# A hybrid S5 / RWKV-7 layer on one core: weight parts made by two streams, S5 matrices set up earlier, v convolved on TensorE, gate blocks moved

## Chip, cores and metric

The kernel runs on one core of a Trainium2 chip. The metric is the device time of one execution in microseconds. A core has five engines: TensorE (PE, with its weight loads as PEld), VectorE (DVE), ScalarE (ACT), GpSimd (POOL) and SyncE (SP, which here issues nearly all DMAs).

## The reference

One layer over a latent stream x (512 tokens of 1024) and a context stream ctx (256 tokens) that share all weights, in fp32. Only x is returned; of the context only the end states of the two recurrences are used.

```python
x   = half_ffn(x,   mod_x, 0, ...)      # SwiGLU, FFN_DIM 2816, x + 0.5*mod*y
ctx = half_ffn(ctx, mod_c, 0, ...)
hc, hx = modulate(ctx, ...), modulate(x, ...)
_, ctx_states = token_mixers(hc, 1, zeros, p, False)
out_x, _ = token_mixers(hx, rows, ctx_states, p, True)
x = x + mod_x[5] * out_x
x = half_ffn(x, mod_x, 2, ...)
return rmsnorm(x, final_g)
```

Inside token_mixers (cut): one product with w_in gives the S5 input u, the RWKV r, k, v, the low-rank inputs of decay and rate, and two gates.

```python
ya = s5_scan(u, forward) + s5_scan(u, backward) + D * u      # 32 groups, 64 complex states
rkv = centred_conv(rkv, conv, rows)          # 3x3 per channel on 8 rows of 64 tokens (context: 1 row)
S = S*w + (S@aa) x bb + v x k ; yb = S@r     # RWKV-7, 8 heads of 64, both directions
ya = gelu(ya); ya = ya * sigmoid(ya @ w_glu)
yb = (group_norm(yb) + bonus) * g @ w_o
out = (sigmoid(gate_a) * (ya @ w_proj) + sigmoid(gate_b) * yb) @ w_out
```

## The kernel before

**Products.** Every weight tile (128 x 1024 fp32, `raw`) comes by DMA and is split in two fp32r parts: `wh` is a rounded copy made on ScalarE, `wl = raw - wh` a subtraction on VectorE or GpSimd. The activations are split alike (`hx` of the latents, `hc` of the context, `ah`/`al` of the FFN's hidden values), and each product is three matmuls (`mm3`): hi x wh, lo x wh, hi x wl. In the instruction rows hx_109 and hx_110 are the two parts of the latents. All products stand in one list, `items`: context FFN, latent FFN with the context's w_in products (`win`) between, w_in of the latents, 16 gate blocks, then glu, wo, proj, wout, and the second FFN. `dense` (line 352) walks through the list. Before each item it calls `w_split` (line 328) until the item's tiles and some more (`WLA`, or 2) are split, so casts and subtractions are issued from within the stream of products.

**Order.** The program is written by a planner, `Plan` (line 61), a list scheduler with a cost for each kind of operation. Each stage is a generator, a stream with a priority; at each `yield` it names what it needs next (tiles, or events that another stream posts), and `run` takes the first stream by priority that is ready by the plan's clock. Every operation is issued from one helper (line 209), so that all rows of the profile have that line and are told apart by tile. `shared` (line 103) keeps one list of intervals in which VectorE and GpSimd use a common port, and lays operations of both after each other.

**Stages.** `phase_a` runs the modulation products (w_mod), both first FFNs and, in `ctx_run` (line 908), the context's mixers. `s5_build` (line 955) computes the S5 transfer matrices: powers of the state matrix on VectorE, 96 products and sums on GpSimd (tiles ms, X), others on VectorE (mh, H), then 16 rounds on TensorE, each with four transposes of X and four products of X with cb, copied out on ScalarE and stored by DMA (GTd, Kd). It is added as a stream in `ctx_run`, after the context FFN. The context recurrence needs its event `s5b`. `rw_pre`, `rw_main` (lines 1577, 1641) do RWKV in chunks: steps 0 to 3 for the context, 4 to 11 for the latents (tiles T, tt, M, w, R, Z, bt); `s5_rec` (line 1747) the S5 recurrence on GpSimd, four small operations a chunk.

**Before the recurrence of the latents.** `conv_evac` and `conv` (lines 1229, 1243) make the 3x3 convolution: each w_in product of r, k, v is copied into a zeroed 10x66 tile `pad`, scaled by the centre tap, and eight scalar-tensor-tensor operations on VectorE add the other taps (tiles cvr, cvk, cvv). `pa` and `pb` (lines 1291, 1371) make the chunk operands: nb, kt, st.

**After it.** `s5_out`, then `s5_post`: yi is loaded back, gelu gives `yg`, on which `glu_mm` (line 1888) waits. Of the 16 gate blocks the last four stand after glu (`GLUP`). `wo_mm` and `proj_mm` (lines 1874, 1906) work on halves of the tokens; each loads its gate tile `gt` (two buffers) just before its products.

Of the kernel before, what the change touches and what calls it, by code (L numbers as in the profile page):

```python
# [17 lines left out]
FT = 22  # L18
# [10 lines left out]
SPD = 0  # L29
WOL = 4  # L30
S5V = 600
S5Q = 3000
MPV = 1200
SPLIT_AT = 0
S5P = 3
# [6 lines left out]
WLA = 4  # L42
GLUP = 4
# [8 lines left out]
class Plan:  # L52
# [8 lines left out]
    def __init__(self, nc):  # L61
# [5 lines left out]
        self.port, self.shape = [], None  # L67
# [35 lines left out]
    def shared(self, t, cost):  # L103

        self.port = [i for i in self.port if i[1] > min(self.free["V"], self.free["P"])]
        for a, b in self.port:
            if t + cost <= a:
                break
            t = max(t, b)
        self.port = sorted(self.port + [(t, t + cost)])  # L110
        return t

    def step(self, e, cost, out, ins, work=0.0, port=False):
# [4 lines left out]
        if port:  # L118
            t = self.shared(t, cost)
# [153 lines left out]
class Reg:  # L273


    def __init__(self, v, n, p0):
# [4 lines left out]
        self.cv, self.kn, self.pd, self.cvq, self.n_conv = {}, {}, {}, [], 0  # L281


class Kern:
# [43 lines left out]
    def w_split(self):  # L328

        nc, i = self.nc, self.n_split  # L330
        if i == len(self.items):
            return
        s = next((s for s in self.slots if i < self.end[s[0]]), None)
        if s is None:
            return
        if i not in self.raw:
            self.w_loads(1)
        self.n_split += 1
        nb = self.items[i][1]
        r, sr = self.raw.pop(i)  # L340
        self.slots.remove(s)
        wh, wl = (s[0].tile([128, 8, 128], F32R, name=n, tag=f"{n}{s[1]}") for n in ("wh", "wl"))
        nc.scalar.copy(wh[:, :nb], r[:, :nb])
        f = self.sch.free
        late = max(f["P"], self.sch.t) + 2300 > max(f["V"], self.sch.t) + 1150
        eng = nc.vector if (i < self.n_post + 2 or i >= self.n_ffn) and late else nc.gpsimd
        eng.tensor_sub(wl[:, :nb], r[:, :nb], wh[:, :nb].bitcast(F32))
        if sr[0] not in self.gone:
            self.raws.append(sr)
        self.wsp[i] = (wh, wl, s)  # L350

    def dense(self):
# [3 lines left out]
        while i < len(self.items):  # L356
# [3 lines left out]
            while self.n_split < i + n:  # L360
                self.w_split()
            self.w_loads()
            la = WLA if self.n_post <= i < self.n_ffn else 2
            for _ in range(la):
                if self.n_split < i + n + la:
                    self.w_split()
            yield list(self.wsp[i][:2])
            ws = [self.wsp[j][:2] for j in range(i, i + n)]
# [8 lines left out]

    def parts(self, px, ws, h, spec):

        for s, ks, c, needs in spec:  # L380
            yield needs + list(ws[s])
# [17 lines left out]
    def build(self):  # L399
        nc, tc, a, es = self.nc, self.tc, self.a, self.es  # L400
        self.X, self.C = X, C = Reg(0, NX, 4), Reg(1, NCT, 0)
        self.raw, self.wsp, self.n_load, self.n_split, self.late = {}, {}, 0, 0, None
# [49 lines left out]
        self.items[i] += (["b2"],)  # L452
        self.n_post = len(self.items)
# [32 lines left out]
    def mods01(self):  # L486
# [11 lines left out]
        def loaded(n):  # L498
# [6 lines left out]
            if n == 12:  # L505
                self.w_loads(2)
            if n == 16:
                self.w_loads()

        def step(n):  # L510
            if n >= 6:
                next(st0, None)
            if n >= 13:
                self.w_split()
# [245 lines left out]
    def tail(self, l, r, ws):  # L760
# [8 lines left out]
        def half(s, c):  # L769
            px = self.dbank()[:, :256]  # L770
            wh, wl = ws[s]
            yield [wh, wl]
# [59 lines left out]
    def down_half(self, l, r, ws, b):  # L832

        nc, v, c = self.nc, r.v, r.half[b]
        for q in range(KT // 2):
            wh, wl = ws[q // 2]
            yield [wh, wl, self.hid[FT - 1][1]]
# [22 lines left out]
    def phase_a(self):  # L860
        nc, a, sch, X, C = self.nc, self.a, self.sch, self.X, self.C
        with ExitStack() as es:
# [4 lines left out]
            C.h = [hcp.tile([128, KT, NCT], F32R, name=f"hc{i}") for i in range(2)]  # L867
            wrs, self.wxr = self.right("wxr")
# [8 lines left out]
            sch.add(self.dn, 9)  # L877
            sch.run(*st)
# [29 lines left out]
    def ctx_run(self, es, wrs):  # L908
# [3 lines left out]
        X.fp = es.enter_context(self.pool("fpx"))  # L912
        sch.post("fp0x")
# [6 lines left out]
        self.cas.close()  # L920
# [1218 lines left out]
```

## Time and profile before

| | us |
|---|---|
| runs | 1901.99, 1898.08, 1900.58 (median 1900.58) |
| profiled execution, its own time | 1891.72 |
| its span | 1890.0 |
| TensorE busy, share | 1672.3, 88% |
| VectorE | 996.4, 53% |
| ScalarE | 716.9, 38% |
| GpSimd | 687.5, 36% |
| mean granted TensorE clock | 0.939 of full speed |

The stages along the span, by the tiles in the trace: 0 to 109 us modulation products; 109 to 273 context FFN; 273 to 857 latent FFN, with the S5 set-up, the context's w_in and preparation, and the context recurrence between; 857 to 1082 w_in of the latents, convolution, pa and pb; 1082 to 1351 gates and latent recurrence; 1351 to 1531 glu, gates, wo, proj, wout; from 1531 the second FFN and the last norm. A share of busy time over the span is a mean over these; the stages are read one by one.

### The profile page before, as it was taken

To read this page: it belongs to the slowest core of one execution; us is meant where nothing else is said; L and a number is where in the kernel's file an instruction comes from. 1 tells how busy PE (TensorE), PEld (TensorE's weight loads), DVE (VectorE), ACT (ScalarE), POOL (GpSimd) and SP (SyncE) were. 2 spreads that over 40 slices of the span, in tenths; PEclk is the share of its full clock that TensorE was granted. 3 is DMA by queue.
4 is the path that set the end of the run, shared out by engine and by line. 5 is a ranking of instruction groups with operands and counts; after the bars stand their busy time and mean duration, and the time that the engine had idled before them with its cause. 6 is when DMAs were issued, how large, how long until landed. Compare 5 with 4: busy or idle time off the path is not lost.

```text
span 1890.0 us, 33157 instructions
## 1 busy us (share of the span) xinstructions
PE 1672.3 (88%) x13208; PEld 1400.3 (74%) x13208; DVE 996.4 (53%) x1747; ACT 716.9 (38%) x1200; POOL 687.5 (36%) x815
## 2 busy tenths in 40 slices
PE   6889999999999988778976789968697999999996
PEld 3689987778878867665544567758587988888886
DVE  3376564755558728355788855643343433333335
ACT  3355442545463212535443333443443332222222
POOL 0144231555764314621334537660065421111111
PEclk9999999999999999888988889979799999999998
DMA  9955541335454474433753566466364223323231
GB/s 310 331 167 195 183 155 57 113 106 159 143 160 140 141 190 151 119 123 128 252 160 105 148 223 188 118 172 176 123 215 159 67 69 101 99 91 101 98 101 56
DMA packets 235626, 278.43 MB, mean 147 GB/s; under 512 B 93616, under 2 KB 186800, under 8 KB 234448
## 3 DMA queue, kind: packets, MB, share of 16 engines
q1 hardware_dynamic: 235472, 276.32, 47.8%
q8 instruction: 104, 1.70, 0.4%
q14 instruction: 50, 0.41, 0.1%
HBM read 234.31 MB, written 43.22 MB: 147 GB/s over the span
## 4 chain that ended last, share of the span: by engine, by line
PE 56%; DVE 14%; DMA 14%; ACT 6%; issue 4%; POOL 3%; SPq 3%; DVEq 0%; ACTq 0%; POOLq 0%
PE b L209 56%; DMA wmod<-in_wmod 3%; SPq L209 3%; POOL wl L209 2%; ACT wh L209 2%; DMA Hd<-H 2%; DMA raw<-in_wgu 2%; DVE st L209 1%; DVE mh L209 1%; DVE wl L209 1%; DMA gt<-gates 1%; DVE rs L209 1%; DVE prod L209 1%; DVE cvr L209 1%; DVE H L209 1%
## 5 line engine op out<-in xcount | busy, mean ns | idle before, releaser
L209 PE MATMUL b<-hx,wh 128*128 128x512 f32 (+1 forms) x2432 | 698.2, 374 | 22.6 <-ACT wh L209 10.9
L209 POOL TENSOR_TENSOR wl<-raw,wh 128x1024 fp32r<-128x1024 f32 x135 | 329.3, 2443 | 822.0 <-ACT wh L209 748.1
L209 PEld LDWEIGHTS b<-hx,wh 128*128 128x128 f32 x2432 | 439.1, 194 | 106.7 <-issue 19.0
L209 PE MATMUL b<-hx,wl 128*128 128x512 f32 (+1 forms) x1216 | 448.6, 369 | 7.6 <-POOL wl L209 6.0
L209 ACT CAST wh<-raw 128x1024 fp32r<-128x1024 f32 x273 | 283.1, 1046 | 196.3 <-DMA raw<-in_wgu 69.8
L209 DVE TENSOR_TENSOR wl<-raw,wh 128x1024 fp32r<-128x1024 f32 x138 | 187.3, 1358 | 276.9 <-ACT wh L209 274.5
L209 PEld LDWEIGHTS b<-hx,wl 128*128 128x128 f32 x1216 | 235.7, 194 | 47.9 <-POOL wl L209 8.6
L209 PE MATMUL b<-ah,wh 128*128 128x512 f32 (+1 forms) x560 | 196.8, 351 | 3.6 <-ACT wh L209 2.0
L209 PE MATMUL b<-ah,wl 128*128 128x512 f32 (+1 forms) x560 | 194.9, 348 | 1.9 <-POOL wl L209 1.9
L209 PE MATMUL b<-al,wh 128*128 128x512 f32 (+1 forms) x560 | 194.7, 348 | 0.0
L209 PE MATMUL b<-hc,wh 128*128 128x256 f32 x928 | 173.1, 287 | 1.2 <-ACT hc L209 1.2
L209 PEld LDWEIGHTS b<-hc,wh 128*128 128x128 f32 x928 | 145.8, 192 | 10.9 <-issue 8.2
L209 PE MATMUL b<-hc,wl 128*128 128x256 f32 x464 | 131.7, 284 | 0.0
L209 PEld LDWEIGHTS b<-ah,wh 128*128 128x128 f32 x560 | 108.0, 193 | 16.6 <-ACT wh L209 2.2
L209 PEld LDWEIGHTS b<-ah,wl 128*128 128x128 f32 x560 | 107.9, 193 | 15.2 <-POOL wl L209 2.1
L209 ACT CAST ah<-prod 128x512 fp32r<-128x512 f32 (+1 forms) x68 | 36.6, 538 | 212.6 <-DVE prod L209 212.5
L209 PEld LDWEIGHTS b<-al,wh 128*128 128x128 f32 x560 | 107.8, 192 | 12.1
L209 ACT ACTIVATE sil<-b 128x512 f32<-128x512 f32 (+1 forms) x68 | 35.0, 515 | 149.8 <-PE b L209 149.6
L209 PEld LDWEIGHTS b<-hc,wl 128*128 128x128 f32 x464 | 89.3, 192 | 0.0
L209 DVE TENSOR_TENSOR prod<-sil,b 128x512 f32<-128x512 f32 (+1 forms) x68 | 39.6, 582 | 93.0 <-PE b L209 74.4
L209 DVE SCALAR_TENSOR_TENSOR x1c<-b,gp,x1c 128x512 f32<-128x512 f32 (+1 forms) x67 | 43.9, 662 | 81.2 <-PE b L209 81.2
L209 PE MATMUL b<-wmod,zs 128*32 128x256 f32 x576 | 54.3, 465 | 19.3 <-DMA wmod<-in_wmod 19.1
(289 smaller groups left out, 2331.0 us busy)
## 6 DMA issues: line engine op xcount, KB each, us to landing
raw<-in_wgu SPq DMA_DIRECT2D x132, 512.0 KB, 3.9
wmod<-in_wmod SPq DMA_DIRECT2D x72, 512.0 KB, 5.3
raw<-in_wdn SPq DMA_DIRECT2D x66, 512.0 KB, 3.7
raw<-in_win SPq DMA_DIRECT2D x49, 512.0 KB, 4.0
gt<-GTd SPq DMA_DIRECT2D x32, 256.0 KB, 3.8
abk<-st SPq DMA_DIRECT2D x8, 1024.0 KB, 5.5
AB<-abk SPq DMA_DIRECT2D x8, 1024.0 KB, 6.3
GTd<-gst SPq DMA_DIRECT2D x16, 256.0 KB, 2.4
```

The costliest lines, as they stand in the source:

```text
L209: r = f(out, *args, **kw)
```

## The change

1. `w_split` goes. Two streams take its place: `w_high` casts each tile on ScalarE as soon as it is loaded and a slot is free, `w_low` subtracts on GpSimd or, if it is ready earlier there, on VectorE; always on VectorE while the flag `rec` is set, that is during the latents' S5 recurrence. `dense` and the other users wait for the event of the split (`whole`). Of 273 splits 212 are on VectorE then and 61 on GpSimd (before 138 and 135).
2. `shared` is rewritten: an operation that would begin within an interval of the other engine waits for its end, and lengthens what the other engine has queued.
3. `s5_build` is added in `phase_a` and has its memory from there; its main loop waits for the end of the modulation loads (`wm`), and its costs in the plan (`S5V`, `S5Q`, `S5P`) change. The stores wait in the stream for their tile.
4. `gate` loads gate tiles two ahead, in four buffers. `glu` stands behind all gate blocks, and the last four blocks wait for the event `step10`, so that they stand beside the last step of the recurrence and ahead of glu. yi has two buffers.
5. For the latents the convolution of v goes to TensorE: `taps` makes nine diagonal matrices with one affine_select on GpSimd, `conv_mm` nine fp32 matmuls into one bank. The pad is a plain 512 tile without border, and `reach` cuts the ranges, for k and r on VectorE as well. There are three pads.
6. In `pa` the tile cm goes (ep is used in place); in `pb` nb, kt and half of st are made on VectorE for the latents, on GpSimd only for the context.

```diff
-S5V = 600
-S5Q = 3000
+S5V = 250
+S5Q = 600
-S5P = 3
+S5P = 6
-GLUP = 4
+WP = 5
+ONPE = "v"
+GLUP = 0
...
-    def w_split(self):
...
+    def w_high(self):
+        yield ["load"]
+        for i in range(len(self.items)):
+            while True:
+                self.w_loads()
+                s = next((s for s in self.slots if i < self.end[s[0]]), None)
+                if i not in self.raw:
+                    yield [f"split{i - 1}"]
+                elif s is None:
+                    yield [f"free{min(self.wsp)}"]
...
+            self.nc.scalar.copy(wh[:, :nb], r[:, :nb])
...
+    def w_low(self):
...
+            v, p = (max(sch.free[e], sch.t) for e in "VP")
+            eng = nc.vector if self.rec or p + 2300 > v + 1150 else nc.gpsimd
+            eng.tensor_sub(wl[:, :nb], r[:, :nb], wh[:, :nb].bitcast(F32))
...
+        self.items[-4] += (["step10"],)
...
+            self.sbs, sb = self.right("sb")
...
+            sch.add(self.w_high(), WP)
+            sch.add(self.w_low(), WP)
+            sch.add(self.s5_build(sb), S5P)
...
-        self.sbs, sb = self.right("sb")
-        sch.add(self.s5_build(sb), S5P)
...
+            if name in ONPE:
+                self.taps(r, ch)
+                r.cvq.append((n, ch))
+                return
...
+    def conv_mm(self, r):
...
+        for i, t in enumerate((4, 0, 1, 2, 3, 5, 6, 7, 8)):
+            o, i_ = self.reach(t)
+            self.nc.tensor.matmul(o3[o], dg[:, t], i3[i_], start=i == 0, stop=i == 8, skip_group_check=True)
...
+                B = Pg if r.v else V
...
-                Pg.tensor_mul(nb, fw(nkk, d), ic)
+                B.tensor_mul(nb, fw(nkk, d), ic)
...
+    def gate(self, n):
+        order = [(h, m + 2 * t + e) for h in range(2) for m in (8, 0) for t in range(4) for e in range(2)]
+        while len(self.gts) < min(n + 3, len(order)):
+            h, d = order[len(self.gts)]
+            self.gts.append(self.c1.tile([128, 256], F32, name="gt", bufs=4))
+            self.nc.sync.dma_start(self.gts[-1], self.gates[d][:, self.X.half[h]])
+        return self.gts[n]
...
-            g = self.cp.tile([128, 256], F32, name="gt", bufs=2)
-            nc.sync.dma_start(g, self.gates[8 + d][:, c])
+            g = self.gate(16 * h + d)
```

In the rows below, out<-in are the tiles of a matmul (b is a PSUM bank), then its shape. On TensorE the four transposes that begin a round of the S5 set-up (`ident,X`) stand before among the products of the latent FFN:

```order
L209 MATMUL b_4035<-hx_110,wh 128x512
L209 MATMUL b_4035<-hx_109,wl 128x512
L209 MATMUL b_4053<-ident,X 128x128 x4
L209 MATMUL b_4035<-hx_109,wh 128x512
L209 MATMUL b_4035<-hx_110,wh 128x512
```

In the changed kernel the first ones stand among the products of the context FFN (`ah`, `al`), whose tiles have 256 columns:

```order
L212 MATMUL b_1444<-al,wh 128x256
L212 MATMUL b_1444<-ah,wl 128x256
L212 MATMUL b_1455<-ident,X 128x128 x4
L212 MATMUL b_1444<-ah,wh 128x256
L212 MATMUL b_1444<-al,wh 128x256
```

All 16 rounds are moved in this way, from between weight products 1965 and 2709 (counted from the start) to between 366 and 1269.

The context recurrence on TensorE, a step of it from the product T,M to Z,M, before:

```order
L209 MATMUL b_7832<-T_7758,M 32x32 x16
L209 MATMUL b_7866<-tt_7148,w 32x32 x16
L209 MATMUL b_7888<-ident,AB 128x128 x4
L209 MATMUL b_7894<-ident,AB 128x128 x4
L209 MATMUL b_7908<-Z_7160,M 64x64 x16
```

And in the changed kernel, from the end of the nine weight products that follow T,M in the second step to those that follow Z,M:

```order
L212 MATMUL b_7095<-hx_109,wh 128x512
L212 MATMUL b_7095<-hx_110,wh 128x512
L212 MATMUL b_7095<-hx_109,wl 128x512
L212 MATMUL b_7145<-tt_6480,w 32x32 x16
L212 MATMUL b_7167<-ident,AB 128x128 x4
L212 MATMUL b_7173<-ident,AB 128x128 x4
L212 MATMUL b_7187<-Z_6492,M 64x64 x16
L212 MATMUL b_7095<-hx_109,wh 128x512
L212 MATMUL b_7095<-hx_110,wh 128x512
```

There the latent FFN's products hx,wh and hx,wl stand in the pauses of the step; the recurrence begins at weight product 2970 instead of 3480.

TensorE at the passage from the latents' recurrence to glu, before: the last products of the S5 output (hs,gt), a transpose of sg, the product for RWKV's g (sgd,g) and the first rows of glu (`yg`):

```order
L209 MATMUL b_14020<-hs,gt 64x64
L209 MATMUL b_14021<-hs,gt 64x64
L209 MATMUL b_14065<-ident,sg_13963 128x128 x4
L209 MATMUL b_14088<-sgd,g_11013 128x256 x2
L209 MATMUL b_14140<-yg_14082,wh 128x512
L209 MATMUL b_14140<-yg_14083,wh 128x512
```

In the changed kernel, the end of the last recurrence step (Z,bt; M,Z; AB,Z) and what follows it:

```order
L212 MATMUL b_13905<-ident,sg_13839 128x128 x4
L212 MATMUL b_13915<-Z_13505,bt 64x64 x16
L212 MATMUL b_13937<-M,Z_13505 64x64 x16
L212 MATMUL b_13937<-AB,Z_13504 64x64 x16
L212 MATMUL b_13972<-hx_109,wh 128x512
L212 MATMUL b_13972<-hx_110,wh 128x512
```

The four gate blocks (96 products of hx) now begin here, and glu's first product stands behind them.

## Rows read from the trace of the kernel before

**Rows 1.** The page: busy time, share of the span and instructions of each engine.

```profile
PE 1672.3 (88%) x13208; PEld 1400.3 (74%) x13208; DVE 996.4 (53%) x1747; ACT 716.9 (38%) x1200; POOL 687.5 (36%) x815
```

**Rows 2.** Table of stretches: stretch, its length, busy times, granted TensorE clock, DMA.

```profile
core 0: us, PE busy (x) PEld busy (x) DVE busy (x) ACT busy (x) POOL busy (x), PEclk, DMA share, GB/s
0.00:109.00 109.00, 82.65 (x660) 56.04 (x660) 41.84 (x110) 38.22 (x75) 14.18 (x20) 0.98 0.90 296
109.00:273.00 164.00, 161.65 (x1355) 161.21 (x1355) 104.46 (x146) 83.14 (x124) 63.92 (x34) 0.99 0.57 184
...
300.00:735.00 435.00, 412.97 (x2386) 340.16 (x2384) 267.71 (x497) 171.90 (x289) 203.01 (x191) 0.97 0.50 143
735.00:857.00 122.00, 92.62 (x1237) 83.79 (x1234) 65.12 (x146) 51.22 (x106) 58.74 (x142) 0.87 0.39 111
857.00:1082.00 225.00, 176.77 (x1247) 118.26 (x1247) 167.40 (x230) 96.11 (x150) 87.90 (x71) 0.86 0.53 161
1082.00:1351.00 269.00, 217.34 (x3455) 179.89 (x3453) 129.62 (x242) 102.93 (x204) 113.96 (x281) 0.87 0.57 166
...
1531.00:1890.00 359.00, 343.60 (x1603) 288.53 (x1602) 126.10 (x186) 90.05 (x119) 55.68 (x28) 0.98 0.30 94
```

**Rows 3.** The same table for three short stretches.

```profile
1240.00:1256.00 16.00, 1.98 (x46) 1.61 (x48) 5.39 (x14) 3.02 (x4) 14.20 (x47) 0.57 0.40 127
1330.00:1351.00 21.00, 7.42 (x17) 3.44 (x17) 4.05 (x6) 9.77 (x17) 1.26 (x1) 0.60 0.35 89
750.00:806.00 56.00, 40.55 (x815) 35.29 (x816) 23.09 (x49) 26.84 (x50) 39.29 (x121) 0.88 0.40 100
```

**Rows 4.** TensorE, groups by shape, 320 to 470 us: busy us, mean ns, idle before.

```profile
L209 PE MATMUL b<-cb,X 128*128 128x32 f32 x64 | 8.1, 270 | 2.6 <-DVE cb L209 2.6
L209 PE MATMUL b<-ident,X 128*128 128x128 f32 x32 | 5.3, 292 | 0.0
```

**Rows 5.** Weight splits: tile wl on VectorE; both timelines near 107 us; the page.

```profile
L209 DVE TENSOR_TENSOR wl<-raw,wh x138: 1207/1226/2584, 30.6 to 1847.7; 128x1024 fp32r<-128x1024 f32 x138
...
107.81 2.27 DVE L209 TENSOR_TENSOR wl<-raw,wh 128x1024 fp32r<-128x1024 f32 x1 [1.73 <-ACT wh L209]
111.99 0.86 DVE L209 SCALAR_TENSOR_TENSOR mt<-x,A,b 128x256 f32<-128x256 f32 x2
...
106.65 2.35 POOL L209 TENSOR_TENSOR wl<-raw,wh 128x1024 fp32r<-128x1024 f32 x1 [15.76 <-ACT wh L209]
111.87 2.40 POOL L209 TENSOR_TENSOR wl<-raw,wh 128x1024 fp32r<-128x1024 f32 x1 [2.88 <-ACT wh L209]
...
L209 PE MATMUL b<-hx,wl 128*128 128x512 f32 (+1 forms) x1216 | 448.6, 369 | 7.6 <-POOL wl L209 6.0
```

**Rows 6.** Tiles ms, X and mh: count, then duration in ns, least/median/most.

```profile
L209 POOL TENSOR_TENSOR ms<-pz,hb x64: 637/658/1636, 347.9 to 541.0; 128x256 f32<-128x256 f32 x64
L209 POOL TENSOR_TENSOR X<-ms x32: 726/742/1599, 349.6 to 541.7; 128x256 f32<-128x256 f32 x32
...
L209 DVE TENSOR_TENSOR mh<-pw,hc x64: 400/418/2626, 348.3 to 661.0; 128x256 f32<-128x256 f32 x64
```

**Rows 7.** VectorE groups, 857 to 1082 us, and TensorE's timeline at 927 us.

```profile
L209 DVE SCALAR_TENSOR_TENSOR cvv<-pad,cw,cvv 128x512 f32<-128x512 f32 x32 | 31.2, 976 | 0.8
...
927.01 1.02 PE L209 MATMUL b<-vs,flip 128*128 128x512 f32 x2
```

**Rows 8.** VectorE, 857 to 1082 us, and GpSimd, 857 to 1351, by shape.

```profile
L209 DVE TENSOR_TENSOR st<-nb,em 64x512 f32<-64x512 f32 x7 | 9.9, 1420 | 0.0
L209 DVE TENSOR_TENSOR ks<-ks,cvr 128x512 f32<-128x512 f32 x3 | 2.1, 684 | 0.0
...
L209 POOL TENSOR_TENSOR nb<-kkr,ic 128x512 f32<-128x512 f32 x8 | 12.8, 1595 | 23.8 <-ACT kkr L209 14.2 <-ACT kt L209 6.9 <-DMA bond<-ks 2.7
```

**Rows 9.** Waits, 1082 to 1351 us, then 1390 to 1455: total us, times, longest.

```profile
PE b L209 <- ACT yg L209: 11.1, 3, 6.8
...
PE b L209 <- DVE gt L209: 5.8, 4, 2.3
PE b L209 <- DVE gb L209: 5.0, 6, 2.4
```

More of the change, by code (lines that the diff above doesn't have):

```diff
@@ L41 @@
 QHI = 6000
-WLA = 4
-GLUP = 4
+WP = 5
+ONPE = "v"
+GLUP = 0
 UAT = 3
@@ L118, in step @@
         if port:
-            t = self.shared(t, cost)
+            t = self.shared(e, t, cost)
         if e == "T":
@@ L326, in w_loads @@
             most -= 1
-    def w_split(self):
[L330 to L350, printed above, removed]
+    def w_high(self):
[8 more added lines that the diff above has]
+                    yield [f"free{min(self.wsp)}"]
+                else:
+                    r = self.raw[i][0]
+                    if self.sch.ready(r) <= self.sch.t + 60:
+                        break
+                    yield [r]
+            nb = self.items[i][1]
+            self.slots.remove(s)
+            wh, wl = (s[0].tile([128, 8, 128], F32R, name=n, tag=f"{n}{s[1]}") for n in ("wh", "wl"))
+            self.nc.scalar.copy(wh[:, :nb], r[:, :nb])
+            self.wsp[i] = (wh, wl, s)
+            self.item[wh.tensor.name] = i
+            self.sch.post(f"high{i}")
+            yield
@@ new lines, in w_low @@
+    def w_low(self):
+        nc, sch = self.nc, self.sch
+        for i in range(len(self.items)):
+            yield [f"high{i}"]
+            wh, wl, _ = self.wsp[i]
+            yield [wh]
+            nb, (r, s) = self.items[i][1], self.raw.pop(i)
+            v, p = (max(sch.free[e], sch.t) for e in "VP")
+            eng = nc.vector if self.rec or p + 2300 > v + 1150 else nc.gpsimd
+            eng.tensor_sub(wl[:, :nb], r[:, :nb], wh[:, :nb].bitcast(F32))
+            if s[0] not in self.gone:
+                self.raws.append(s)
+            self.w_loads()
+            sch.post(f"split{i}")
+            yield
@@ L359, in dense @@
                 yield self.items[i][4]
-            while self.n_split < i + n:
-                self.w_split()
             self.w_loads()
[L363 to L366, printed above, removed]
+            yield [f"split{i}"]
             yield list(self.wsp[i][:2])
+            yield [f"high{j}" for j in range(i, i + n)]
             ws = [self.wsp[j][:2] for j in range(i, i + n)]
@@ L376, in dense, with whole @@
             yield
+    def whole(self, w):
+        return [f"split{self.item[w[0].tensor.name]}"] + list(w)
     def parts(self, px, ws, h, spec):
         for s, ks, c, needs in spec:
-            yield needs + list(ws[s])
+            yield needs + self.whole(ws[s])
             for k in ks:
@@ L1193, in win_mm @@
             self.win_evac(r, m, px)
+        if r.cvq and not (M_R <= m < M_WD and self.cv_name(m) in ONPE):
+            yield from self.conv_mm(r)
     def rot(self, dst, src):
@@ L1909, in proj_mm @@
             d = 2 * t + e
-            g = cp.tile([128, 256], F32, name="gt", bufs=2)
-            nc.sync.dma_start(g, self.gates[d][:, c])
+            g = self.gate(16 * h + 8 + d)
             px = self.dbank()[:, 0:256]
```

129 lines of the change are left out of this document (84 added, 45 removed).

## The prediction

> **What bounds the kernel now.** I read the page's busy times first: TensorE is busy for 1672.3 of 1890.0 us and VectorE for 996.4, with ScalarE and GpSimd below that [rows 1]. So TensorE is the engine to watch, and what can be won is the 218 us in which it stands idle and the time in which it runs at less than its full clock. The table by stage [rows 2] tells where these lie; in each row the reader is to compare the busy time of PE with the length of the stretch, and to look at the granted clock. From 109 to 273 us (the context stream's first FFN) PE is busy for 161.65 of 164 us at clock 0.99, and from 1531 us on (second FFN) for 343.60 of 359: nothing is free there. The gaps are in 735 to 857 (92.62 of 122, clock 0.87: the context recurrence), 857 to 1082 (176.77 of 225, clock 0.86: conv and RWKV preparation of the latents, where VectorE is busy for 167.40) and 1082 to 1351 (217.34 of 269, clock 0.87: latent recurrence). The third view cuts out three short stretches [rows 3]: 1240 to 1256, PE busy 1.98 us, clock 0.57; 1330 to 1351, 7.42 of 21 us, clock 0.60; and 750 to 806, 40.55 of 56, clock 0.88. A clock of 0.57 means that most of the stretch was at 1.2 instead of 2.4 GHz, after PE had stood nearly still. The change aims at each of these gaps and pays for it in the full stretch from 109 to 273 us.
>
> The profiled execution took 1891.7 us; the median of the three runs is 1900.6, that is 8.9 us more. The sum is made against 1891.7 and the 8.9 are added at the end.
>
> **S5 matrices early: what the full stretch pays.** 16 rounds of transposes and kernel products move from under the latent FFN into the context FFN. In the trace 8 rounds (64 and 32 matmul records, [rows 4]) take 8.1 + 5.3 = 13.4 us of PE, so 16 take 27. Where they stood PE was busy for 412.97 of 435 us and the other work will close up; where they go it is full. So: **+27 there, -27 later**; this sums to nothing, but moves work from a stretch with gaps to one without.
>
> Their elementwise work moves along. GpSimd gets about 60 of the 64 products at 0.66 us and 30 of the 32 sums at 0.74 [rows 6], 39.5 + 22 = 62 us, and 5 more weight splits at 2.40 [rows 5], 12 us; it goes from 63.92 to 138 us, and fits into 164 + 27 = 191. VectorE gets some 70 operations on 128x256 at 0.42 [rows 6], 29 us, and 64 small copies, at most the same 0.42 each, 27 us, on 104.46: about 160 of 191. Each fits by itself. But the two disturb each other: a split on VectorE takes 1.23 us as a rule and took 2.27 us at 107.81 us, when a split of GpSimd (2.35 us from 106.65) was running [rows 5]; it ended 1.08 us after that one's end, nearly its own length later. So count both as users of one resource: GpSimd's 138, VectorE's 28 splits (34 us) and its 70 operations (29 us) make 201 us, against 191 us of PE. It is just full, and a queue that is just full makes PE wait for some wl. Bounds: nothing, if the planner packs them; +40, if only 0.87 of the time is usable. I take **+13**, nearer to the lower end, since PE stood 6.0 us in all behind GpSimd's wl in the FFN products and win [rows 5], and splits can be made ahead.
>
> The new split streams (the cast on ScalarE, then the subtraction) let weights be ready during the first 109 us, where DMA is at 0.90 and PE at 82.65 of 109 [rows 2]; more raw tiles can be consumed between the modulation loads, but those loads limit it: **-5** (-10 to +5). The stretch to 273 us together: +27 + 13 - 5 = **+35** (+17 to +72).
>
> The Trainium skill (page "SBUF — State Buffer", section "Who interferes with whom") says that a VectorE instruction with two SBUF inputs and a GpSimd instruction that reads SBUF exclude each other for a whole instruction. By that rule the 201 us cannot overlap anywhere, and the time is that of rival (a) or (c) below. The 2.27 us row agrees with it; no row shows it for the small S5 operations.
>
> **The context recurrence between FFN products.** Before, its four steps have no weight product between their small matmuls, as the order shows; with the S5 matrices done it starts 510 products sooner (counted along PE's order, 2970 against 3480) and takes six or nine products into each pause. The idle time and the lost clock in 300 to 735 are 22 us and 3% of 413 = 12; in 750 to 806 they are 15.5 us and 12% of 40.6 = 5 [rows 2, 3]. Of these 54 us I take 60%, **-33** (-12 to -50): the waits of the norm that follows, and the pauses between the last steps, stay. What is late next is the end of the latent FFN itself, which is PE work. With the -27 from above: **-60**.
>
> **v convolved on PE.** 32 scalar-tensor-tensor operations of 31.2 us leave VectorE [rows 7]; 32 operations of the RWKV preparation come from GpSimd, where such a one takes 1.60 us, and on VectorE one half as wide took 1.42 [rows 8], although another operation on 128x512 (ks) took 0.68. That is 32 x 0.68 = 22 to 32 x 1.42 = 45 us on VectorE, less the blocking that GpSimd's absence ends (its conv operations took 0.98, on the same 128x512). I get about 140 of 167 us. PE gets 4 x 9 = 36 fp32 matmuls over at most 512 columns. The nearest row is an fp32 128x512 matmul, two records of 1.02 us together [rows 7]: 37 us, up to 74 at half the clock. Work of PE here at full clock is 176.77 x 0.86 = 152; with 37, 189. Now the stretch is 225 long because VectorE sets it. If PE waits less, its clock stays higher: 189 / 0.95 + 6 us of waits = 205, so **-20** (-45, if VectorE sinks to 140 and PE's own products fill all; +10, if the nine matmuls run at the low clock and nothing is taken off the path).
>
> **The four gate blocks, the gates' loads, the recurrence.** In 1330 to 1351 PE does 7.42 us of work, waiting for yi and then yg (6.8 us at longest [rows 9]). Four blocks of 24 products that stood after glu now cover that; at 343.60 us for 1603 matmuls in the second FFN [rows 2], 0.21 each, they last 21 us: **-13** (the whole gap would be -13.6). From 1240 to 1256 PE waits for the recurrence's inverse; GpSimd, which makes S5's scan at that time, no longer gets splits there, so s5_out can fill in: **-8** (0 to -14). Loads two products ahead end the waits that stand as PE behind gt and gb, 5.8 and 5.0 us in 1390 to 1455 [rows 9]: **-10** (-4 to -13). The recurrence's start is earlier by 72 products: **-5** (0 to -10). The price: after glu no gate block covers the last step of the RWKV output, on which wo waits: **+4** (0 to +15). Together **-32** (-10 to -50). For the loads, SP's queue gets the three loads ahead of the next raw tile; they wait for a free buffer, and the raw loads behind them are a few blocks ahead, so nothing is charged.
>
> **The second FFN**: PE is at 343.60 of 359 [rows 2], splits move from GpSimd to VectorE, which has 233 us free: **0**.
>
> **Sum**: +35 - 60 - 20 - 32 = -77; 4 us go back for new waits that I cannot place: -73. 1891.7 - 73 = 1818.7, and 8.9 more on the scale of the runs: **1828 us**.
>
> **Rivals.** (a) *The shared resource costs more.* The 201 us cannot be packed and PE waits for wl in the context FFN: 201 / 0.87 = 231 against 191, +40 instead of +13: 1855 us. For it speaks the 2.27 us row; against it that PE hardly waits for wl today. (b) *All covers hold.* +17 to 273 us; -77 in place of -60; -40 for the conv; -45 in place of -32: -145, 1756 us. For it speaks that every gap named is idle time; against it, that gaps of a chain rarely close completely. (c) *Slower: the S5 set-up holds up the splits.* VectorE's 160 and GpSimd's 138 us run one after the other, because each blocks the other and the streams of the planner wait for one another: 298 us where 191 are needed, +107, and with the 27 and -5 a stretch of +129. The rest gives -60 - 20 - 32 + 4 = -108, so +21 in all: 1922 us. It decides from +108 in this stretch on. Against it speaks that not all of VectorE's work stretches: two of mt, which read a PSUM bank beside SBUF, took 0.86 us together while GpSimd ran a split [rows 5]. (d) *The change doesn't do what it says.* The products between the recurrence steps wait for weights, and the gate blocks come when yg is there already; only the moves of work remain: +35 - 27 = +8, 1909 us. Against it: the planner's order has the products in place.
>
> **How the numbers follow.** Forecast 0.58, (a) 0.18, (b) 0.11, (c) 0.08, (d) 0.05. The forecast's own range has all four terms halfway to their better ends (-9 - 8 - 12 - 9: 1790) or to their worse ones (+18 + 10 + 15 + 11: 1882). The range takes this in with (a), and half of the way on to (b) and some us of spread above; (c), (d) and (b) stay out of it: **1774 to 1888**. A measurement of this kernel can tell 0.2%, that is 3.8 us. Faster: forecast, (a) and (b) with 0.87; (c) and (d) are slower, less 0.03 for cases that meet in between: faster 0.87, same 0.03, slower 0.10.
>
> **What would show it.** Right: the context FFN ends 25 to 50 us later than 273; no stretch with clock below 0.95 between 300 and 800 us; the hx products stand between T,M and R,tt matmuls; in the conv stage PE at a clock above 0.92 and dg matmuls near 1 us a matmul; no PE wait for yg; DVE's waits for gt<-gates gone. Wrong: a context FFN longer by over 70 us with PE waiting for wl (a, c), a conv stage no shorter than 225 us, or a new wait of wo for yb after glu of more than 15 us.

## The result

The changed kernel takes 1912.35 us in the median of six runs (1911.13 to 1923.30), the kernel before 1899.78 in the six runs beside it; the ratio is 1.006, with a 95% interval of 1.0033 to 1.0087. So it is **slower by some 12 us, 0.6%**, where 1828 and a gain of 72 were forecast. The profiled execution has a span of 1910.5 us at a mean clock of 0.947, against 1890.0 and 0.939. These two traces lie 20 us apart where the medians lie 12.6 apart, since the trace of before is of one of its faster executions; what is read from single traces below is good to some us only.

### The profile page after: what moved, and what is told of

It reads as the page before. It is cut to its first block, busy times and chain, and to the rows that moved or that the text cites. A ratio compares the mean times of both kernels' runs of the same rounds, so it can differ in the third digit from the quotient of the medians.

```text
span 1910.5 us, 33149 instructions
## 1 busy us (share of the span) xinstructions
PE 1710.8 (90%) x13280; PEld 1420.2 (74%) x13280; DVE 1046.7 (55%) x1821; ACT 707.6 (37%) x1192; POOL 481.5 (25%) x711
## 5 line engine op out<-in xcount | busy, mean ns | idle before, releaser
L212 DVE TENSOR_TENSOR wl<-raw,wh 128x1024 fp32r<-128x1024 f32 x212 | 269.8, 1279 | 202.7 <-ACT wh L212 199.8
L212 POOL TENSOR_TENSOR wl<-raw,wh 128x1024 fp32r<-128x1024 f32 x61 | 151.7, 2496 | 319.4 <-ACT wh L212 290.8
L212 PE MATMUL b<-ah,wh 128*128 128x512 f32 (+1 forms) x560 | 201.2, 359 | 8.7 <-DVE c L212 6.2
L212 PE MATMUL b<-hc,wh 128*128 128x256 f32 x928 | 183.6, 298 | 8.5 <-DVE c L212 5.7
L212 PEld LDWEIGHTS b<-hc,wh 128*128 128x128 f32 x928 | 152.7, 201 | 18.7 <-issue 12.5
L212 PE MATMUL b<-hc,wl 128*128 128x256 f32 x464 | 135.8, 293 | 4.8 <-POOL wl L212 4.3
L212 PEld LDWEIGHTS b<-al,wh 128*128 128x128 f32 x560 | 108.8, 194 | 12.6 <-DVE al L212 0.3
L212 POOL TENSOR_TENSOR acc<-acc,sq 128x256 f32<-128x256 f32 x12 | 8.8, 736 | 377.3 <-ACT sq L212 377.3
L212 PEld LDWEIGHTS b<-hc,wl 128*128 128x128 f32 x464 | 93.2, 201 | 5.7 <-POOL wl L212 4.9
```

Source lines behind the costliest of these rows:

```text
L212: r = f(out, *args, **kw)
```

## The profile after

The page of the changed kernel, busy times first (compare [rows 1]):

```profile
PE 1710.8 (90%) x13280; PEld 1420.2 (74%) x13280; DVE 1046.7 (55%) x1821; ACT 707.6 (37%) x1192; POOL 481.5 (25%) x711
```

TensorE is busy for 38.5 us more (1710.8 against 1672.3), and VectorE for 50; GpSimd has lost 206. The work moved as the order said. What the stretches give is read from the matmuls with a weight part (`wh` or `wl`), of which every kernel here has 7152. The table gives the time, in us from the span's start, at which the matmul after the first n of them begins, in the last row the last one (the last columns are experiments that follow):

```
   n   before  after   e1    e5    e7    e10   e12
 200      99     86    94    86    88    86    90
1584     269    342   264   313   304   311   310   first of the latent FFN
3672     836    873   841   846   842   844   833   first of w_in of the latents
4200    1109   1124  1091  1098  1090  1100  1085   first gate block
4632    1389   1407  1374  1379  1370  1389  1363   first of wo
5400    1503   1521  1485  1491  1484  1500  1475   first of the second FFN
last    1874   1895  1861  1866  1860  1876  1849
```

In the first 100 us the changed kernel gains 13. Between product 200 and the latent FFN, in the context FFN, it loses 86, and stands 73 behind. It wins 36 back up to w_in of the latents, and 22 more up to the gate blocks; from there to the second FFN it loses 3, and in the second FFN 2. So the change became slower in one stretch, and a second one, that of the gates and the latent recurrence, gave nothing. How far single traces can be trusted is seen from e2, e3, e4, e8 and e9, which have the same order of work as the changed kernel up to the latent FFN: their traces reach it at 341.7 to 349.7 us.

The table of stretches, from 100 us to the first product of the latent FFN (341.9 us; before it was 268.8, compare the second of [rows 2]):

```profile
core 0: us, PE busy (x) PEld busy (x) DVE busy (x) ACT busy (x) POOL busy (x), PEclk, DMA share, GB/s
100.00:341.90 241.90, 205.81 (x1587) 198.56 (x1587) 164.97 (x262) 93.44 (x157) 152.28 (x137) 0.92 0.57 167
```

PE is busy for 205.81 of 241.90 us at clock 0.92, where it had 161.65 of 164 at 0.99. The S5 rounds are in it with these two groups, by shape (compare [rows 4], where 8 rounds stand), and after them what TensorE waited for, and what VectorE waited for longest:

```profile
L212 PE MATMUL b<-cb,X 128*128 128x32 f32 x128 | 17.3, 281 | 3.9 <-DVE cb L212 3.9
L212 PE MATMUL b<-ident,X 128*128 128x128 f32 x64 | 12.0, 293 | 12.2 <-POOL X L212 12.2
...
DVE H L212 <- DMA Hd<-H: 30.4, 8, 5.9
PE b L212 <- POOL X L212: 12.2, 7, 2.8
PE b L212 <- DVE c L212: 11.8, 3, 5.7
PE b L212 <- POOL wl L212: 4.3, 3, 2.0
PE b L212 <- DVE cb L212: 3.9, 4, 1.7
```

The matmuls of the 16 rounds take 29.3 us; 27 were forecast. TensorE's idle time in the stretch is 36.1 us, most of it in waits: for X, made on GpSimd, 12.2 us; for c, made on VectorE, 11.8. From 100 to 268.8 us it was 4.0 before. What is left of the 73 us, some 12, is TensorE's other work at the lower clock. And VectorE itself stood for 30.4 us, eight times, until a **store** of H had read its tile (DMA Hd<-H). The kernel before had that wait as well, 17.4 us in the latent FFN:

```profile
DVE H L209 <- DMA Hd<-H: 17.4, 10, 4.8
```

One of these in the timeline, VectorE first, then TensorE, then the table of four short stretches around it:

```profile
177.29 1.93 DVE L212 TENSOR_TENSOR H<-mh 128x256 f32<-128x256 f32 x1 [4.13 <-DMA Hd<-H]
179.14 3.35 DVE L212 TENSOR_TENSOR wl<-raw,wh 128x1024 fp32r<-128x1024 f32 x1
182.42 0.86 DVE L212 SCALAR_TENSOR_TENSOR c<-b,gp,c 128x256 f32<-128x256 f32 x2
...
183.04 0.77 PE L212 MATMUL b<-hc,wh 128*128 128x256 f32 x2 [5.65 <-DVE c L212]
...
176.59 4.83 POOL L212 TENSOR_TENSOR wl<-raw,wh 128x1024 fp32r<-128x1024 f32 x2
```

```profile
170.00:177.00 7.00, 7.00 (x61) 7.00 (x60) 3.15 (x5) 2.62 (x5) 6.16 (x8) 1.00 0.54 159
177.00:183.00 6.00, 0.38 (x4) 0.14 (x2) 5.71 (x4) 1.79 (x3) 6.00 (x4) 0.76 0.03 4
183.00:187.00 4.00, 3.96 (x19) 3.99 (x19) 3.92 (x8) 0.00 (x0) 3.55 (x5) 0.50 0.85 270
187.00:191.00 4.00, 4.00 (x36) 4.00 (x36) 1.63 (x8) 1.57 (x3) 0.00 (x0) 1.00 0.65 213
```

H has one buffer. From 173.2 us VectorE waits for the store of the last H (4.13 us), then runs the 1.93 us of H and a split, and only then c, which stands behind in its fixed order, though PE had ended its products for c by 177.4 us, when it began to wait. PE waits 5.65 us for c. After this it runs at 0.50, that is at 1.2 GHz, from 183 to 187 us: the stall is paid and then part of it again. Not every stall is followed by such time: from 187 to 217 us, with a wait of 2.05 us for X in it, the clock is 1.00. The split took 3.35 us instead of 1.23, while GpSimd ran two splits from 176.59 to 181.42 and then the products ms.

Of the places that were to gain: no wait for yg is left [rows 9]. From 1395 to 1475 us the waits behind gt and gb are down to 2.6 and 2.1 us, and a wait of wo for yb came, 6.0 us, after glu:

```profile
PE b L212 <- ACT yb L212: 6.0, 1, 6.0
PE b L212 <- DVE gt L212: 2.6, 4, 1.1
PE b L212 <- DVE gb L212: 2.1, 3, 1.1
```

The wait for yb ends with the first product of wo, at 1407.3 us, and behind it the clock is 0.50 again:

```profile
1407.30:1414.00 6.70, 5.87 (x22) 4.88 (x22) 3.21 (x6) 2.78 (x4) 1.13 (x1) 0.50 0.45 138
```

From the first gate block to the first product of wo, before and then after, TensorE is idle for nearly the same time, 46.1 and 45.4 us:

```profile
1108.60:1389.20 280.60, 234.54 (x3297) 194.81 (x3296) 139.71 (x262) 114.74 (x208) 116.80 (x267) 0.90 0.55 161
```

```profile
1123.70:1407.30 283.60, 238.21 (x3418) 195.74 (x3416) 136.32 (x249) 115.11 (x218) 105.43 (x262) 0.93 0.57 173
```

But it waits for other things. The longest waits there, before and then after, beside the 6.0 us for yb (T<-ti is the load of the recurrence's inverse, AB and U are loads of the two recurrences' operands, gt of S5 matrices; for gt it waited before as well, 4.3 us just ahead of this stretch):

```profile
PE b L209 <- DMA T<-ti: 16.5, 4, 12.5
PE b L209 <- ACT yg L209: 13.3, 4, 6.8
```

```profile
PE b L212 <- DMA AB<-abk: 8.1, 5, 2.3
PE b L212 <- DMA U<-udx: 5.5, 2, 5.0
PE b L212 <- POOL hs L212: 5.1, 1, 5.1
PE b L212 <- DMA gt<-GTd: 5.0, 5, 2.8
```

## The experiments

All are made from the changed kernel or, from e13 on, from e12. The kernel before took 1903 to 1906 us in the median beside them, so that ratios are compared. The planner writes the whole program anew for each edit, so that an edit can also move work that it doesn't name.

**e1: S5 late.** The stream of the S5 set-up and its pool go back into `ctx_run`, with the old constants (`S5V`, `S5Q`, `S5P`) and PSUM bank; to make room, the latent FFN's pool is opened earlier and one cast waits for an event. The main part of the edit:

```diff
-            self.sbs, sb = self.right("sb")
...
-            sch.add(self.s5_build(sb), S5P)
...
+        self.sbs, sb = self.right("sb")
+        sch.add(self.s5_build(sb), S5P)
```

> The changed kernel with its S5 set-up put back where it was (after the context FFN, with the old constants and memory order), the weight streams, conv, gates left as changed. Theory (the S5 rounds and their VectorE/GpSimd work in the context FFN cost the 73 us by which the latent FFN begins later, and give 40 back up to the conv): the latent FFN begins at 262 to 275 us, the whole takes about 1870 to 1885 us, faster than both kernels. Rival (the new split streams, which give VectorE more splits, slow the context FFN): the latent FFN still begins later than 300 us and the whole stays above 1900. Second rival (S5 early does pay for itself through the recurrence): slower than 1912.

Measured: 1871.92 us, ratio 0.983 (0.980 to 0.986); the latent FFN begins at 264.5 us. This is the theory's number. The rest of the change is worth 1.7%, and the early S5 set-up makes it slower by 2.3%. The new split streams do not slow the context FFN (its end is 264.5 us, before 268.8).

**e2: v convolved on VectorE** (`ONPE = ""`).

> The changed kernel with v convolved on VectorE again (the unpadded conv with cut ranges, all else as changed). Theory (the conv on PE gives some 16 us between the end of the latent FFN and the latent recurrence): 1923 to 1935 us. Rival (that stretch shortened for another reason, the halves of st, nb and kt moved off GpSimd): 1908 to 1916.

Measured: 1917.01, ratio 1.0073 (1.0049 to 1.0096) against 1.006 (1.0033 to 1.0087) with v on PE. It is not the theory's number, and just above the rival's; the intervals lie over each other. From the first product of w_in of the latents to the first gate block this run takes 253.1 us, the changed kernel 250.2 and the kernel before 272.4. The stretch did not shorten because of the conv.

**e3: the last gate blocks behind glu** (`GLUP = 4`, no step10).

> The changed kernel with the last four gate blocks behind glu again, without the wait for step10; gates still loaded two ahead. Theory (the blocks cover the wait for yi and gelu before glu, but their lack afterwards opens one before wo, so that the move is worth nothing): 1908 to 1918 us, with PE waiting for yg again some 10 us and not for yb. Rival (the move gains its 13 us, and another part lost them): 1922 to 1930.

Measured: 1914.84, ratio 1.0042 (1.0014 to 1.007): the theory's time; the move is worth nothing that can be told. But TensorE waits only 1.1 us for yg here, not 10.

**e4: gate tiles loaded at use**, two buffers.

```diff
-        while len(self.gts) < min(n + 3, len(order)):
+        while len(self.gts) < min(n + 1, len(order)):
...
-            self.gts.append(self.c1.tile([128, 256], F32, name="gt", bufs=4))
+            self.gts.append(self.c1.tile([128, 256], F32, name="gt", bufs=2))
```

> The changed kernel with each gate tile loaded at its use again, two buffers. Theory (the loads ahead remove most of the waits behind gt, 11 us of PE waits before and 5 now): 1918 to 1924 us. Rival (the waits were covered by other work, or the gates' loads only moved): 1909 to 1915.

Measured: 1928.02, ratio 1.0119 (1.0088 to 1.0151): slower by 0.6% than the changed kernel, 11 us. The loads ahead are worth what the prediction put on them (10), measured against loads at use in the changed kernel.

The next three ask what in the early set-up costs.

**e5: the products one round later.** Each round's transposes and products are issued after the next round's GpSimd operations, and hk, which they need, has a third buffer:

```diff
+            if prev:
+                yield from product(*prev)
+            prev = X, Ct, d, h2
+        yield from product(*prev)
```

> The changed kernel with the TensorE part of each S5 round (four transposes, four products, their stores) issued one round later, after GpSimd's operations of the next round; the work is the same. Theory (PE, in its fixed order, stands behind X because GpSimd's operations take longer than planned, 12 us in the trace, and runs at the lower clock after each stall): the latent FFN begins at 310 to 325 us instead of 342, PE's wait for X is under 3 us, the whole takes 1885 to 1900 us. Rival (GpSimd and VectorE are simply full in this stretch, and all that PE does waits for them, through wl, c or prod in the place of X): the latent FFN still begins at 335 us or later, the whole takes 1906 to 1916.

Measured: 1883.21, ratio 0.9897 (0.9847 to 0.9946); the latent FFN begins at 312.6 us, PE's wait for X is 1.6 us. In the stretch the theory's numbers, in the total 2 us below its range: the same work costs 31 us less when PE takes X later. VectorE still waits 25.3 us for the stores of H.

**e6: X only once** (the other 15 rounds use the X of the first; 90 of 96 GpSimd operations left out).

> The changed kernel in which GpSimd makes X only in the first S5 round; the other 15 rounds use the same X (90 of 96 GpSimd operations, some 65 us of its time, are left out). Theory: without them neither X waits nor the mutual blocking of GpSimd and VectorE remain, the context FFN pays the 27 us of PE work and little else; the latent FFN begins at 295 to 310 us and the whole takes 1865 to 1885. Rival (the cost is the PE work, VectorE's 70 operations and 64 copies, not GpSimd's): it begins at 325 us or later, and the whole takes 1895 or more.

Measured: 1888.46, ratio 0.9913 (0.9884 to 0.9942), the latent FFN at 323.5 us: between the two. With GpSimd's work gone, VectorE still stood 39.1 us behind the stores of H, and PE 12.4 behind c. So GpSimd's load alone isn't the cost: with 65 us of it left out less is won in this stretch (18 us) than in e5 (29), where all of it stays.

**e7: H late.**

```diff
+            yield ["dl0c0"]
             nxt = load(0, "hc", a["s5C"])
```

> The changed kernel in which only the S5 rounds stay early; VectorE's products for H (tiles mh and H, 96 operations, 54 in the context FFN) begin after the context FFN. Theory (GpSimd's X decides, VectorE's part is the smaller one): the latent FFN begins at 325 to 338 us, the whole takes 1900 to 1910 us. Rival (VectorE's operations with two SBUF inputs are what blocks GpSimd and holds up c and prod): it begins before 315 us, the whole takes 1880 to 1895.

Measured: 1876.20, ratio 0.9847 (0.9801 to 0.9893), the latent FFN at 304.1 us. The theory is refuted: without VectorE's part in this stretch 38 of the 73 us are gone, more than without GpSimd's in e6. The latent FFN now begins 35 us later than before, which is the prediction's own term for this stretch, though that counted VectorE's part in.

**e8: splits during the S5 recurrence by the general rule** (`rec` stays False).

> The changed kernel in which the weight splits during the latents' S5 recurrence go to GpSimd or VectorE by the general rule again. Theory (the S5 recurrence on GpSimd began late and ended at 1268 us, 6 us later than before, so keeping GpSimd free for it bought nothing): 1908 to 1918 us. Rival (the flag is worth the 8 us that the prediction put on it): 1918 to 1926.

Measured: 1933.20, ratio 1.0137 (1.0077 to 1.0198): slower by 0.8%, 15 us, than the changed kernel. The theory is refuted, though the size is uncertain, as the two intervals just overlap. The rule puts 7 splits on GpSimd during the S5 recurrence of the latents, which then takes 113 us there instead of 100. In its trace, whose execution took 1946.81 us, the way from the first gate block to wo takes 303.7 us, in that of the changed kernel 283.6.

**e9: nb, kt and half of st on GpSimd** (`B = Pg`).

> The changed kernel with nb, kt and the half of st made on GpSimd again for the latents. Theory (v's convolution on PE alone was worth nothing measurable in its own run; the 20 us that the stretch from the end of the latent FFN to the S5 input gained come from taking these operations off GpSimd, where one takes 1.60 us): 1922 to 1935 us. Rival (they cost VectorE what they cost GpSimd; the gain comes from the weight streams): 1908 to 1917.

Measured: 1929.87, ratio 1.0135 (1.0116 to 1.0155): 14 us slower, the theory's number. The rows show why. VectorE's operations with nb, from 900 to 1120 us, first in this run, then in the changed kernel:

```profile
L212 DVE TENSOR_TENSOR st<-nb,em 64x512 f32<-64x512 f32 x8 | 12.3, 1540 | 0.0
```

```profile
L212 DVE TENSOR_TENSOR st<-nb,em 64x512 f32<-64x512 f32 x16 | 10.9, 683 | 0.2
```

Eight half tiles take 12.3 us beside GpSimd, and sixteen take 10.9 without it: 1540 against 683 ns each. Taking over the other half of these cost VectorE nothing. In all, from the first product of w_in of the latents to the first gate block, VectorE is busy for 173.29 us here with 242 operations, and for 169.55 in the changed kernel with 273. The Trainium skill (page "SBUF — State Buffer", section "Who interferes with whom") has it that a VectorE instruction with two SBUF inputs contends with a GpSimd instruction that reads SBUF; these rows agree.

**e10: H in three half buffers**, stored as soon as it is made, all S5 work still early.

```diff
-                H, ms = half("H"), half("mh")
+                ms = half("mh")
...
+                    H = sb.tile([128, 256], F32, name="H", bufs=3)
```

> The changed kernel in which H has three buffers of half its size, each stored as soon as it is made, and all S5 work stays early. Theory (VectorE stands 30 us behind the stores of H, since H has one buffer and VectorE's order is fixed; behind it wait c, prod and the splits, and PE behind them): VectorE's wait for Hd<-H under 8 us, the latent FFN begins at 305 to 320 us instead of 342, the whole takes 1878 to 1895. Rival (it is the number of VectorE's operations with two SBUF inputs beside GpSimd's, not the wait for the store): it begins at 330 us or later, 1900 to 1913.

Measured: 1885.88, ratio 0.9899 (0.9857 to 0.9941), the latent FFN at 310.6 us; no wait for Hd<-H is left. The theory's numbers: the number of VectorE's operations with two SBUF inputs in this stretch, which the rival had, is not smaller here, but larger (splits, mh and H are 100, in the changed kernel 81). PE still waits 10.0 us for X. But the planner has moved something else too: GpSimd makes fewer of the weight splits between 100 us and the latent FFN. The splits on GpSimd there, in the changed kernel, e6, e10 and e12:

```profile
L212 POOL TENSOR_TENSOR wl<-raw,wh x25: 2344/2405/2842, 100.9 to 336.6; 128x1024 fp32r<-128x1024 f32 x25
```

```profile
L212 POOL TENSOR_TENSOR wl<-raw,wh x27: 2332/2419/2644, 102.0 to 310.9; 128x1024 fp32r<-128x1024 f32 x27
```

```profile
L212 POOL TENSOR_TENSOR wl<-raw,wh x12: 2372/2432/3414, 102.0 to 266.6; 128x1024 fp32r<-128x1024 f32 x12
```

```profile
L212 POOL TENSOR_TENSOR wl<-raw,wh x6: 2370/2420/2676, 104.7 to 297.0; 128x1024 fp32r<-128x1024 f32 x6
```

In e5 and e7 there are 12 too. So each run with S5 early that wins 29 us or more in this stretch also has half or more of GpSimd's splits there moved to VectorE, and e6, which has not, wins least (18). No run moves the splits alone, and this rival stays open.

**e11: e7 and e5 together.**

> H after the context FFN and TensorE's part of each S5 round one round later, together. Theory (two separate stalls, VectorE behind H's stores and PE behind X, each with its time at the lower clock): the latent FFN begins at 288 to 300 us, 27 us of S5 work on PE later than without it, and the whole takes 1862 to 1875 us. Rival (the two are the same stall, seen twice): no better than H late alone, 304 us and 1873 to 1880.

Measured: 1872.22, ratio 0.9829 (0.981 to 0.9847), the latent FFN at 299.1 us. These are the theory's numbers, but the gain over e7 (0.9847) is not told, and 5 us of the stretch are within the spread of single traces: e12, e13, e14 and e15 below have the same order of work up to the latent FFN and reach it at 305.0 to 311.0. So this run doesn't show two separate stalls.

**e12: e10 and e5 together** (hk is loaded in its own round, in two buffers). Nothing is left out or moved back; in the edit only the buffers and the round differ from the changed kernel, and by the planner's choice the splits.

> H in three half buffers and TensorE's part of each S5 round one round later; all S5 work stays in the context FFN. Theory: the latent FFN begins at 290 to 305 us; the whole takes 1862 to 1880 us. Rival (GpSimd and VectorE full, as the prediction's sum of 201 us against 191 had it): it begins at 312 us or later, as with the round later alone, and 1880 to 1890 us.

Measured: **1867.05 us, ratio 0.9813** (0.9789 to 0.9837), the fastest whole version. In the total the theory's number; but the latent FFN begins at 309.6 us, above its 305 and not told from e10's 310.6. By then more of the work is done, though: 50 of the 64 products mh, in e10 38 and in e5 26. The total gains 16 us over e10 and as much over e5, with the intervals apart; in the trace 10 of them over e10 are there at w_in of the latents (833.4 and 844.1). The stretch of the context FFN in e12, then in e7:

```profile
100.00:309.60 209.60, 195.89 (x1618) 189.03 (x1617) 178.83 (x318) 94.18 (x159) 109.17 (x117) 0.98 0.70 204
```

```profile
100.00:304.10 204.10, 195.38 (x1602) 188.35 (x1601) 137.28 (x230) 94.38 (x158) 120.76 (x123) 0.97 0.65 188
```

The columns are those of the table above. PE is busy for 196 and 195 us, 93 and 96% of the stretch, and is here the bound again, at clock 0.98 and 0.97.

**e13: the latents' second inverse cut to 3 of 31 columns** (the rest of it left out), from e12.

> The version with H in three half buffers and the S5 products one round later (1867 us), in which the second inverse of the latents (for the last four recurrence steps) is cut to 3 of its 31 columns on VectorE, so that it is ready early; the rest of it is left out. Theory (the recurrence's last four steps wait for that inverse, which now lands at 1278 us instead of 1248, and this eats what the loads ahead and the free GpSimd give between recurrence and second FFN): 1840 to 1855 us, with the first products of step 8 at least 20 us sooner after those of step 7. Rival (the S5 chain on GpSimd and its output set the time there, the inverse is hidden): 1862 to 1870 us.

Measured: 1864.93, ratio 0.9786 (0.974 to 0.9833), the rival's number. Step 8's first products come 9 us after step 7's Z,bt instead of 37, but the gain is not told from e12: the intervals overlap. The S5 output (hs,gt) ends at 1288.4 us here and at 1289.7 in e12. The inverse is a wait, but the S5 chain ends hardly earlier without it.

**e14: e12 with the gate blocks behind glu.**

> The same version (1867 us) with the last four gate blocks behind glu again. Theory (the move is worth nothing, as it was on the changed kernel): 1862 to 1872 us. Rival (with the earlier stalls gone, it gains the 13 us that the prediction put on it): 1876 to 1884 us.

Measured: 1869.63, ratio 0.9821 (0.9778 to 0.9865): nothing that can be told from e12, again.

**e15: e12 with v on VectorE.**

> The same version (1867 us) with v convolved on VectorE again. Theory (PE's 36 matmuls cost it what VectorE's 32 operations cost the stretch; as on the changed kernel, within 5 us): 1863 to 1873 us. Rival (the conv on PE is worth 10 us or more): 1877 us or more.

Measured: 1872.07, ratio 0.9844 (0.9797 to 0.989): 5 us above e12, as the theory had it, and not told from it. By e2's interval the conv on PE gives less than about 10 us, if anything; by this run's alone it could be 16.

## Why the prediction was wrong, step by step

**The first 109 us**: -5 forecast (-10 to +5), -13 at product 200. The sign was right, the gain larger than the range.

**S5 set-up in the context FFN**: the 27 us of PE were right (29.3). The step that failed is the +13 beside it, with its reason. Between product 200 and the latent FFN 86 us were lost where 40 were forecast, so that this term measured some 57. The 201 us of work of VectorE and GpSimd were counted as a sum of busy times on a shared resource, and its bounds (0 to +40) were bounds of throughput. Such a sum does not set the time: GpSimd's busy time with VectorE's splits, mh and H makes 165 us in e6, whose stretch from 100 us to the latent FFN lasts 223.5, and 218 us in e12, whose stretch lasts 209.6. What the runs show in its place are waits in a fixed order. VectorE stood behind a store for 30.4 us with c, prod and splits queued behind it, and PE stood behind X and c with products queued behind it, and some of these stalls were followed by time at 1.2 GHz (clock 0.92 in the stretch, 0.98 in e12). The stretch came out at +73 instead of +35. The wait of VectorE for Hd<-H was in the trace of before, 17.4 us at its old place, where PE had other products to do. It moved with the work, and the prediction moved only the operations, not their waits. With both stalls mended and all S5 work early (e12) the latent FFN begins 41 us later than before, with H late (e7) 35: the sum was close for a stretch without them.

What each part costs is not shown. Either edit alone gains 31 us, though in e5 VectorE still waits 25.3 us for the stores and in e10 PE still waits 10.0 us for X, and both together gain 47; and with each of them the planner moved splits from GpSimd to VectorE. So rivals (a) and (c) named the place, but the wait that they and the signs of being wrong named, PE behind GpSimd's wl, is 4.3 us. Whether the two engines exclude each other in these operations, as (c) had it, the sums above can't tell, as an instruction that is held up counts as busy (1540 against 683 ns in e9).

**The recurrence between products**: -60 forecast (with the -27). From the first product of the latent FFN to w_in of the latents the changed kernel wins 36. In e1, where the same streams run with S5 late, that stretch is 9 us longer than before; so the early set-up is worth 45 there. In e12 44 are won against before. Right in kind, 16 to 24 too much.

**v on PE**: -20 forecast, with the reason that VectorE's 31.2 us leave, and 22 won up to the first gate block. The number was right, but not the reason, and so it is luck in part: with v back on VectorE (e2) 19 of the 22 are still won. PE's part was costed right: 36 matmuls, two records of 539 ns each in the median. What the runs can tell is the part that the prediction counted as a cost, the 32 operations taken from GpSimd: they give 14 us (e9), half of them in this stretch, since VectorE's own ran at half speed beside them. That term had the wrong sign. The cut ranges of the conv, the third pad and the split streams, which could have given the rest, have no run of their own.

**Gates and the latent recurrence**: -32 forecast, and nothing won: from the first gate block to the second FFN it is 394.0 us before and 396.8 after. This is the second step that failed. The waits that it named are gone, T<-ti from 16.5 to 2.5 us and yg from 13.3 to none, but others of the same sum came in their place (loads of AB and U, hs, gt, yb), for which it had only the +4 behind glu: it took each wait as if nothing stood behind it. By parts: the loads ahead (-10) were right, 11 in e4; and in e3, with the four blocks back at their place, the way from wo to wout takes 57.7 us where it was 66.3 before. The four blocks (-13) were worth nothing in two runs: the wait for yg is gone, but 6.0 us for yb came, and with the lower clock behind it the way from wo to wout is 66.0 us again (clock 0.91). The free GpSimd (-8) made the S5 recurrence of the latents shorter, 100 us instead of 153, but it begins at 1168 us instead of 1110 and ends at 1268 instead of 1264; the 15 us of e8 are measured against 7 splits in it, where the kernel before had 5. "72 products earlier" (-5) is no gain, as those products are still to be done in the stretch; the RWKV recurrence begins at 1174 instead of 1168, and its last AB,Z ends at 1376 instead of 1319. Why the S5 recurrence begins so late stays open (in e2 and e9 it begins 6 us after the first gate block, in the changed kernel 44); the second inverse is late too (its last operation on VectorE begins at 1273.5 instead of 1245.4), and e13 shows that it is waited for, but not that it alone sets the time.

**Second FFN**: 0 forecast, 2 us longer.

The forecast's direction was lost on the S5 term: with its stalls mended (e12) the kernel gains 1.9%, 36 us, where 72 were forecast. Of the 36 that still lack, the traces have most in the gates and the latent recurrence (4 won instead of 32) and in the recurrence between products (44 instead of 60).

## What to carry to other kernels

When work is moved into a full stretch, its waits are moved with it: list what each of its instructions waited for where it stood (a store that still reads the only buffer, above all), and what would then stand behind it in the fixed order of its engine. A sum of busy times cannot show such a cost. Three half buffers in place of one and one round of distance between producer and consumer, with the splits that the planner moved along, turned a change that lost 0.6% into one that gains 1.9%. And before a wait is booked as a gain, name what the engine would wait for next: here 27 us of the named waits of TensorE went, and as much came from others.

## What was unexpected in the hardware

A stall of PE of 5.65 us was followed by 4 us of work at a granted clock of 0.50. Where the stalls were many, the clock of the whole stretch was 0.92, and where they were mended, 0.98. And VectorE did sixteen operations with two SBUF inputs in less time (10.9 us) than eight beside GpSimd (12.3 us).
